# Down-projection weight sums moved from VectorE to copies and accumulating DMAs inside DRAM

## The chip, the core and the metric

The kernel runs on one core of a Trainium2 chip. The metric is the device time of one execution in microseconds. Of the kernel before, three runs gave a median of 1559.25 us (1559.11 to 1559.95). One more execution was profiled, and all views quoted here are of that one.

## The reference

Two layers over 512 tokens and 1024 channels, all in float32. The down-projection at the end of each layer is what the change touches.

```
for l in range(DEPTH):                       # DEPTH = 2
    h = _rmsnorm(x, g_mix[l])
    proj = h @ w_in[l]                       # 1024 -> 6656: gates and the inputs of four branches
    y_a, y_b, y_c, y_d = conv, neighbourhood, dilated and window attention branches (256 wide each)
    branch = jnp.einsum('bsnc,ncd->bsnd', ys, w_branch[l])
    mixed = jnp.sum(gates * branch, axis=2)
    x = x + mixed @ w_out[l]
    # ConvFFN: norm, up-projection to 2 x 2816, conv of width 3, SwiGLU, down-projection
    x = x + _conv_ffn(_rmsnorm(x, g_ffn[l]), w_up[l], ffn_conv_w[l], ffn_conv_b[l], w_down[l])
return x
```

## The kernel before, in words

Every product is made from two parts of each operand (a rounded "hi" and the remainder "lo") in three matmuls per tile. Weights come from one packed DRAM tensor `W`. `weights` loads a unit of 128x1024 into `w_raw` from SP's queue; ScalarE (ACT) makes `w_hi` from it and VectorE (DVE) makes `w_lo`. Two or three units are in hand at a time, so the matrix engine (PE) lives from what ACT and DVE have just converted.

A layer has these stages: a mixing stage (token-major projections for the three attentions, the conformer's GLU, the gates and branches, with attention and convolution steps run beside them by `tick`), the output projection, and the feed-forward stage (`ffn`, then `down`). The norm's reciprocal root `rstd` is needed in two layouts. `finish_norm` turns it: `row<-rstd` writes it to DRAM (L358), `raw<-row` reads it back broadcast to all partitions (L362), and ACT copies it to `RB` (L366). Both DMAs are issued from GpSimd's (POOL's) queue. The other early work of POOL is the rotary embedding of the dilated attention's queries and keys (`qk_stats`, L510 to L513), which DVE then scales (L519).

`down` is a fast matrix product of Winograd's kind: of the 22 tiles of `w_down` it takes pairs, 11 of them (NP2), each pair with four 512-wide blocks b11, b12, b21, b22, and needs four sums of these blocks beside the blocks themselves. `load_quad` (L971) loads a pair's 1 MB with two DMAs from POOL into `quad`; `weight_sums` (L975 to L984) makes four subtractions on DVE in the feed-forward stage and stores the four results `sums` to DRAM, 256 KB each, again from POOL. `last_units` lists what `down` loads as weights: `quad(j, q)` from `W` and `sums(j, a, b)` from that scratch.

The program's order on each engine is set by a scheduler ahead of time; on the chip an engine runs its own list in order. `issue_after(last_mm)`, which `tick` uses around side work, ties only the instructions that run on the engine of `last_mm`, which is PE.

Of the kernel before, what the change touches and what calls it, by code (L numbers as in the profile page):

```python
# [14 lines left out]
F32 = mybir.dt.float32  # L15
# [3 lines left out]
ALU = mybir.AluOpType  # L19
# [3 lines left out]
P = 128  # L23
L = 2
D = 1024
S = 512
# [3 lines left out]
NF = DFF // P  # L30

NP2 = NF // 2

EARLY = (3, 6, 10, 13, 17, 20)
EPS = 1e-6
# [153 lines left out]
class Trunk:  # L189
# [482 lines left out]
        return wait()  # L672


    def attention(self, kind, V, yi):


        nc = self.nc
        v = nc.vector
# [103 lines left out]
        es, n = {}, len(items)  # L783
# [106 lines left out]
    def ffn(self, l, last):  # L890
        nc = self.nc
        v = nc.vector
        U = []
        for i in range(4):
            u = self.conv_tile(f"U{i}")
            nc.gpsimd.memset(u[:, 0:1], 0.0)
            nc.gpsimd.memset(u[:, 513:514], 0.0)
            U.append(u)
        F, self.got = [], {}
        self.load_quad(l, 0)  # L900
        for i in range(NF):
            ys, pss = [], []
            for s in range(2):
                pss.append(self.mm())
                self.block(pss[s])
                self.tick()
            if i % 2 == 0:

                with self.tc.issue_after(self.last_mm.ins):
                    self.weight_sums(l, i // 2)  # L910
            for s in range(2):
                c = i + s * NF
                ps = pss[s]
                u = U[(2 * i + s) % 4]
                v.tensor_tensor(u[:, 1:513], ps, self.RB, ALU.mult)  # L915
                y = self.fp.tile([P, S], F32, name=f"cy{s}", tag=f"cy{s}", bufs=2)
                w = lambda t: self.par('ffn_conv_w', c * 3 + t)
                nc.scalar.activation(y, u[:, 1:513], AF.Identity, scale=w(1), bias=self.par('ffn_conv_b', c))  # L918
                v.scalar_tensor_tensor(y, u[:, 0:512], w(0), y, ALU.mult, ALU.add)  # L919
                v.scalar_tensor_tensor(y, u[:, 2:514], w(2), y, ALU.mult, ALU.add)  # L920
                ys.append(y)
                if s == 0:
                    si = self.fp.tile([P, S], F32, name="fth", tag="fth", bufs=2)
                    nc.scalar.activation(si, y, AF.Silu)  # L924
                    ys[0] = si
            f = ys[1]
            if last and i % 2 == 1 and i // 2 < KT:
                self.turn_res(i // 2)

            fl = self.fp.tile([P, S], F32, name=f"fl{i}", tag=f"fl{i}", bufs=1)  # L930
            v.tensor_tensor(fl, f, ys[0], ALU.mult)
            F.append(fl)
            if i in EARLY:
                self.split_pair(F, EARLY.index(i), self.got)
        return F
# [19 lines left out]
    def last_units(self, l):  # L955

        quad = lambda j, q: self.quads[l][j][:, q * S:(q + 1) * S]
        sums = lambda j, a, b: self.sums[l][j][:, a * S:b * S]
        units = []
        for j in range(NP2):  # L960
            units.append(lambda j=j: [quad(j, 0), sums(j, 0, 1)])
            units.append(lambda j=j: [sums(j, 1, 3)])
        for f in (lambda j: quad(j, 2), lambda j: sums(j, 3, 4), lambda j: quad(j, 3)):
            units.extend(lambda f=f, js=js: [f(j) for j in js] for js in PHASES)
        self.w_list.extend((0, u) for u in units)

    def load_quad(self, l, j):

        self.quad = [self.fp.tile([P, 1024], F32, name="quad", tag="w_more", bufs=2) for _ in range(2)]
        for q in range(2):  # L970
            self.nc.gpsimd.dma_start(self.quad[q], self.quads[l][j][:, q * 1024:(q + 1) * 1024])  # L971

    def weight_sums(self, l, j):

        v = self.nc.vector  # L975
        (b11, b12), (b21, b22) = ((t[:, :S], t[:, S:]) for t in self.quad)
        t3, t2 = (self.fp.tile([P, S], F32, name=n, tag=n, bufs=1) for n in ("t3", "t2"))
        self.after_mm(v.tensor_tensor(t3, b22, b12, ALU.subtract))  # L978
        v.tensor_tensor(b12, b12, b11, ALU.subtract)
        v.tensor_tensor(t2, b22, b12, ALU.subtract)  # L980
        v.tensor_tensor(b21, b21, t2, ALU.subtract)
        self.sums[l][j] = self.dram.tile([P, 4 * S], F32, name=f"sums{j}", tag=f"sums{j}", bufs=1)
        for n, t in enumerate((t2, b12, t3, b21)):
            self.nc.gpsimd.dma_start(self.sums[l][j][:, n * S:(n + 1) * S], t)  # L984
        if j + 1 < NP2:
            self.load_quad(l, j + 1)

    def pair_tags(self, j):

# [15 lines left out]
    def split_pair(self, F, j, got):  # L1005

        nc = self.nc
        v = nc.vector
        fi, fk = F[2 * j:2 * j + 2]

        def tile(t):
            pool = self.xpool if t[:2] in ("xh", "xl") else self.fp
            return pool.tile([P, S], F32R, name=f"p{t}", tag=t, bufs=2 if t in ("lo", "xr", "xn", "cy0", "cy1") else 1)

        tags = self.pair_tags(j)
        ih, kh, il, kl, ah, al = (tile(t) for t in tags[:6])
        if j % 2 == 0:
            got['b'] = [tile(t) for t in tags[6:]]
        lo, hi = slice(0, 256), slice(256, 512)
        bh, bl = (t[:, (lo, hi)[j % 2]] for t in got['b'])  # L1020
        a = self.fp.tile([P, S], F32, name="sum", tag="xr" if j < len(EARLY) else "fth", bufs=2)

        def split(h, l, x):
            nc.scalar.activation(h, x, AF.Copy)
            v.tensor_tensor(l, x, h.bitcast(F32), ALU.subtract)

        v.tensor_tensor(a[:, lo], fi[:, hi], fk[:, hi], ALU.add)
        v.tensor_tensor(fi[:, hi], fi[:, lo], fi[:, hi], ALU.subtract)
        v.tensor_tensor(a[:, hi], a[:, lo], fi[:, lo], ALU.subtract)
        split(ih, il, fi)  # L1030
        split(ah, al, a)
        split(kh, kl, fk)
        v.tensor_tensor(fk[:, lo], fk[:, lo], a[:, hi], ALU.subtract)
        split(bh, bl, fk[:, lo])
        cut = lambda h, l, c: [(h[:, c + b * P:c + (b + 1) * P], l[:, c + b * P:c + (b + 1) * P]) for b in range(2)]
        got[j] = {'a11': cut(ih, il, 0), 's3': cut(ih, il, 256), 'a12': cut(kh, kl, 0), 'a22': cut(kh, kl, 256),
                  's1': cut(ah, al, 0), 's2': cut(ah, al, 256), 's4': cut(bh, bl, 0)}

    def down(self, F, last):
        nc = self.nc  # L1040
        v = nc.vector
# [20 lines left out]
        tags = [f"U{i}" for i in range(4)] + ["cy0", "cy1"] * 2  # L1062
        xt = {(b, h): self.conv_tile(tags[4 * h + b])[:, :S] for h in range(2) for b in range(NB)}
        if last:
            for b, h in ((2, 1), (3, 1), (0, 1), (1, 1), (2, 0), (3, 0), (0, 0), (1, 0)):
                nc.sync.dma_start(xt[b, h], self.resT[b * P:(b + 1) * P, h * S:(h + 1) * S])
            u = [self.fp.tile([P, S], F32, name="xn", tag="xn", bufs=2) for _ in range(2)]
        else:
            u = [xt[0, 1], xt[1, 1]]

            xr = [self.load_res(d, self.fp, f"e{d}" if d < 6 else "xr") for d in range(KT)]

        def add(t, x):
            v.tensor_tensor(t, t, x, ALU.add)
# [2 lines left out]
            nc.scalar.activation(u[b], A[b], AF.Copy)  # L1077
        for b in range(2):
            add(u[b], B[b])
        for b in range(2):  # L1080
            if last:
                add(xt[2 + b, 1], C[b])
            else:
                v.tensor_tensor(xt[2 + b, 1], u[b], C[b], ALU.add)
            add(xt[2 + b, 1], E[b])
        if last:
            for b in range(2):
                for t in (xt[2 + b, 1], xt[2 + b, 0], xt[b, 1]):
                    add(t, u[b])
                self.store(xt, 2 + b, 1)  # L1090
        for banks, x, n, h in ((A, 'a12', 0, 0), (E, 'a22', 2, 0), (C, 's4', 0, 1)):

            whole = len(PHASES) - 2 * (banks is C)
            for js in PHASES[:whole]:
# [8 lines left out]
            for b in range(2):  # L1103
# [4 lines left out]
                if last or banks is C:  # L1108
                    with self.first():
                        add(t, banks[b])  # L1110
                elif banks is E:
                    v.tensor_tensor(t, u[b], banks[b], ALU.add)
                else:
                    nc.scalar.activation(t, banks[b], AF.Copy)
                if last:
# [23 lines left out]
    def run(self):  # L1139
        nc, tc = self.nc, self.tc  # L1140
        with ExitStack() as st:
# [5 lines left out]
            self.psum = pool("psum", space=PSUM)  # L1147
            self.dram = pool("dram", space=bass.MemoryType.DRAM)
            self.w_list = []
            self.quads, self.sums = [], []  # L1150
            for l in range(L):
                off, quads = 0, []
                for kind, _, n in UNITS:
# [4 lines left out]
                    else:  # L1158
                        self.w_list.append((n, lambda src=src: [src]))
                self.quads.append(quads)  # L1160
                self.sums.append([None] * NP2)
                self.last_units(l)
            self.w_emitted = self.w_used = 0
            self.first_hi = None
# [45 lines left out]
    def layer(self, l):  # L1210
# [3 lines left out]
        with tc.tile_pool(name="gate", bufs=1, reuse_waits="tile") as self.gp:  # L1214
            with tc.tile_pool(name="attn", bufs=1, reuse_waits="tile") as self.ap:
# [5 lines left out]
                with self.first():  # L1221
                    for _ in self.qk_stats(Q, 4, 4, None):
# [3 lines left out]
                self.tabs = [None] * 4  # L1226
                self.queue(chain(self.na_biases(l, 3 if l else 5), self.qk_norm(Q, 4, 4, 0),
                                 self.attention('na', V, 1)))
                Vd = self.new_V()
                self.project_v(V, Vd)  # L1230
                Q = self.project_qk()
# [96 lines left out]
```

## Time and profile before

| what | value |
|---|---|
| median of three runs | 1559.25 us |
| profiled execution, first to last instruction (its span, the only time it has) | 1556.7 us |
| PE busy | 1550.7 us |
| DVE busy | 1235.9 us |
| ACT busy | 834.7 us |
| POOL busy | 174.8 us |
| PE's granted clock, mean | 0.999 |
| bytes moved by DMA | 244.86 MB, 46.67 MB of it from POOL's queue |

The median is 2.55 us above the span, which is taken as what lies around the instructions. A busy time is the sum of an engine's instruction times; PE's matmuls overlap each other, so its busy share says that it always had work, not that it ran at its peak.

### The profile page before, as it was taken

What the parts mean: (1) busy time and instruction counts of PE and PEld (TensorE: products, weight loads), DVE (VectorE), ACT (ScalarE), POOL (GpSimd) and SP (SyncE); (2) the same over time, 40 slices, a digit from 0 to 9 for tenths busy, and PEclk for the clock granted to TensorE, in tenths of its full rate; (3) what the DMA queues carried; (4) which work ended last, traced back from release to release, by engine and by line L of the source; (5) the groups of instructions that cost most, each with busy time, mean ns of one, the idle gap of its engine ahead of it and who ended that gap; (6) DMA issues with size and microseconds to landing.
All of it is one profiled execution on the core that took longest, in us unless ns stands there. A gap on an engine that the chain in (4) does not pass through costs nothing.

```text
span 1556.7 us, 20353 instructions
## 1 busy us (share of the span) xinstructions
PE 1550.7 (100%) x7122; PEld 1287.2 (83%) x7122; DVE 1235.9 (79%) x2102; ACT 834.7 (54%) x1420; POOL 174.8 (11%) x304
## 2 busy tenths in 40 slices
PE   9999999999999999999999999999999999999999
PEld 8888888888888888888888888888888888888887
DVE  6689988765689997796676899887656899977964
ACT  6778767333445443364457787672434444443643
POOL 0102002122001111100001020022120111111000
PEclk9999999999999999999999999999999999999999
DMA  7632222222645555576555422223226667655674
GB/s 236 192 93 87 83 81 82 95 98 93 215 162 203 192 187 187 202 238 211 188 181 184 117 72 87 74 76 108 95 95 211 194 221 238 202 203 191 219 231 165
DMA packets 103382, 244.86 MB, mean 157 GB/s; under 512 B 27504, under 2 KB 29424, under 8 KB 103280
## 3 DMA queue, kind: packets, MB, share of 16 engines
q1 hardware_dynamic: 89392, 196.37, 39.6%
q0 software_dynamic: 13600, 46.67, 8.5%
q8 instruction: 56, 0.92, 0.2%
q10 hardware_dynamic: 288, 0.52, 0.1%
q14 instruction: 46, 0.38, 0.1%
HBM read 202.63 MB, written 35.66 MB: 153 GB/s over the span
## 4 chain that ended last, share of the span: by engine, by line
PE 94%; DVE 3%; ACT 3%; issue 0%; ACTq 0%; DVEq 0%
PE mm L243 22%; PE mm L244 22%; PE mm L245 22%; PE aux L1048 3%; PE aux L1047 3%; PE aux L1046 3%; PE mm L467 2%; PE mm L469 2%; PE mm L468 2%; PE mm L1047 2%; PE mm L1048 2%; PE mm L1046 2%; PE aux L760 2%; PE aux L737 2%; PE aux L467 1%; PE aux L469 1%
## 5 line engine op out<-in xcount | busy, mean ns | idle before, releaser
L222 ACT ACTIVATE w_hi<-w_raw 128x1024 fp32r<-128x1024 f32 (+1 forms) x305 | 318.6, 1045 | 382.6 <-PE mm L244 218.9
L243 PE MATMUL mm<-xh,w_hi 128*128 128x512 f32 x1280 | 499.5, 390 | 0.0
L244 PE MATMUL mm<-xl,w_hi 128*128 128x512 f32 x1280 | 498.6, 390 | 0.0
L245 PE MATMUL mm<-xh,w_lo 128*128 128x512 f32 x1280 | 498.6, 390 | 0.0
L224 DVE TENSOR_TENSOR w_lo<-w_raw,w_hi 128x1024 fp32r<-128x1024 f32 (+1 forms) x305 | 368.7, 1210 | 83.4 <-ACT w_hi L222 81.3
L245 PEld LDWEIGHTS mm<-xh,w_lo 128*128 128x128 f32 x1280 | 240.3, 188 | 50.7
L243 PEld LDWEIGHTS mm<-xh,w_hi 128*128 128x128 f32 x1280 | 240.3, 188 | 49.1
L244 PEld LDWEIGHTS mm<-xl,w_hi 128*128 128x128 f32 x1280 | 240.3, 188 | 48.7
L836 POOL TENSOR_TENSOR mx<-mx,t 128x512 f32<-128x512 f32 x44 | 66.9, 1530 | 428.0 <-DVE t L835 327.1
L405 DVE SCALAR_TENSOR_TENSOR cv<-cv,prm 128x512 f32<-128x512 f32 x120 | 93.8, 781 | 0.7
L915 DVE TENSOR_TENSOR U<-mm,RB 128x512 f32<-128x512 f32 x88 | 60.0, 686 | 34.9 <-PE mm L245 34.8
L918 ACT ACTIVATE cy<-U,prm 128x512 f32<-128x512 f32 x88 | 70.7, 807 | 30.1 <-DVE U L915 29.9
L806 DVE TENSOR_TENSOR t<-mm,RB 128x512 f32<-128x512 f32 x64 | 43.9, 686 | 47.0 <-PE mm L245 46.8
L467 PE MATMUL mm<-w_hi,xh 128*128 128x512 f32 x192 | 76.4, 398 | 0.4 <-DVE V L595 0.4
L468 PE MATMUL mm<-w_lo,xh 128*128 128x512 f32 x192 | 75.0, 390 | 0.0
L469 PE MATMUL mm<-w_hi,xl 128*128 128x512 f32 x192 | 74.8, 390 | 0.0
L724 ACT ACTIVATE e<-e,rl 128x256 f32<-128x256 f32 (+2 forms) x96 | 57.3, 597 | 21.8 <-DVE rl L723 21.5
L920 DVE SCALAR_TENSOR_TENSOR cy<-U,prm,cy 128x512 f32<-128x512 f32 x88 | 65.5, 746 | 1.3
L919 DVE SCALAR_TENSOR_TENSOR cy<-U,prm,cy 128x512 f32<-128x512 f32 x88 | 65.3, 744 | 0.6 <-ACT cy L918 0.6
L924 ACT ACTIVATE fth<-cy 128x512 f32<-128x512 f32 x44 | 27.8, 632 | 64.1 <-DVE cy L920 64.0
L984 POOL DMA_DIRECT2D sums<-t x44 | 23.9, 544 | 339.4 <-DVE t L978 311.3
L717 ACT ACTIVATE e<-e,nm 128x256 f32<-128x256 f32 (+2 forms) x96 | 57.6, 600 | 2.7
(300 smaller groups left out, 2605.2 us busy)
## 6 DMA issues: line engine op xcount, KB each, us to landing
w_raw<-W SPq DMA_DIRECT2D x223, 512.0 KB, 3.5
quad<-W POOLq DMA_DIRECT2D x44, 512.0 KB, 5.3
w_raw<-W SPq DMA_DIRECT2D x66, 256.0 KB, 3.6
sums<-t POOLq DMA_DIRECT2D x44, 256.0 KB, 3.2
sums<-quad POOLq DMA_DIRECT2D x44, 256.0 KB, 3.8
w_raw<-sums SPq DMA_DIRECT2D x44, 256.0 KB, 3.8
w_raw<-sums SPq DMA_DIRECT2D x22, 512.0 KB, 4.4
res<-xn SPq DMA_DIRECT2D x24, 256.0 KB, 2.0
```

The source lines that it names most:

```text
L222: w = nc.scalar.activation(hi[:, s], raw[:, s], AF.Copy)
L224: nc.vector.tensor_tensor(lo[:, s], raw[:, s], hi[:, s].bitcast(F32), ALU.subtract)
L243: mm(ps, lhsT=wh, rhs=xh, start=start, stop=False)
L244: mm(ps, lhsT=wh, rhs=xl, start=False, stop=False)
L245: self.last_mm = mm(ps, lhsT=wl, rhs=xh, start=False, stop=stop)
L405: self.after_mm(v.scalar_tensor_tensor(acc, u[:, t:t + S], w(t), acc, ALU.mult, ALU.add))
L467: mm(pss[b], lhsT=self.Xh[k][:, t], rhs=hi[:, s], start=k == 0, stop=False)
L468: mm(pss[b], lhsT=self.Xh[k][:, t], rhs=lo[:, s], start=False, stop=False)
L469: self.last_mm = mm(pss[b], lhsT=self.Xl[k][:, t], rhs=hi[:, s], start=False, stop=k == KT - 1)
L1046: mm(ps, lhsT=x[0], rhs=w[0][:, cols], start=start, stop=False, skip_group_check=again)
L1047: mm(ps, lhsT=x[0], rhs=w[1][:, cols], start=False, stop=False, skip_group_check=again)
L1048: self.last_mm = mm(ps, lhsT=x[1], rhs=w[0][:, cols], start=False, stop=stop, skip_group_check=again)
```

## The change

The loads into `quad`, the four subtractions on DVE and the stores of `sums` are removed from the feed-forward stage. In their place, `weight_sums` becomes a generator of 24 DMAs in each layer, all issued from POOL, DRAM to DRAM. The 11 pairs are cut in three chunks of 4, 4 and 3 (CHUNK), so that a DMA moves 512 or 384 rows of 2 KB, 1.05 or 0.79 MB. Column by column, for each chunk: s3 = b12 and s1 = b11 are copied, b11 is accumulated onto s3 and b21 onto s1, then s3 is copied to s2 and b21 accumulated onto it, and s2 is copied to s4 and b22 accumulated onto it. That is 12 copies and 12 accumulating DMAs a layer. The generator is put on the list of side work in the mixing stage through `slowly`, which yields 12 times before it and twice after each DMA. The scratch `sums` has two buffers, so that the two layers do not share one. Since only additions are made, the signs in `split_pair` and `down` change and some blocks change places; the number of matmuls stays as it was.

```diff
+CHUNK = 4
+SLOW = 2
...
+    def slowly(self, g):
+        for _ in range(12):
+            yield
+        for _ in g:
+            for _ in range(SLOW):
+                yield
...
-        self.load_quad(l, 0)
...
-            if i % 2 == 0:
-                with self.tc.issue_after(self.last_mm.ins):
-                    self.weight_sums(l, i // 2)
...
-            units.append(lambda j=j: [quad(j, 0), sums(j, 0, 1)])
+            units.append(lambda j=j: [quad(j, 1), sums(j, 0, 1)])
             units.append(lambda j=j: [sums(j, 1, 3)])
...
+    def weight_sums(self, l):
+        add = self.nc.gpsimd.dma_start
+        items = []
+        for c in range(0, NP2, CHUNK):
+            n = min(CHUNK, NP2 - c)
+            t = self.dram.tile([n * P, 4 * S], F32, name=f"sums{c}", tag=f"sums{c}", bufs=2)
+            self.sums[l].append(t)
+            src = self.all_quads[l][c * P:(c + n) * P]
+            part = lambda x, i: x[:, i * S:(i + 1) * S]
+            items.append((part, t, src))
+        s2, s1, s3, s4 = range(4)
+        b11, b12, b21, b22 = range(4)
+        for d, s in ((s3, b12), (s1, b11)):
+            for part, t, src in items:
+                add(part(t, d), part(src, s))
+                yield
+        for d, s in ((s3, b11), (s1, b21)):
+            for part, t, src in items:
+                add(part(t, d), part(src, s), accum_op=ALU.add)
+                yield
+        for d, b, s in ((s2, s3, b21), (s4, s2, b22)):
+            for part, t, src in items:
+                add(part(t, d), part(t, b))
+                yield
+            for part, t, src in items:
+                add(part(t, d), part(src, s), accum_op=ALU.add)
+                yield
...
-        v.tensor_tensor(fk[:, lo], fk[:, lo], a[:, hi], ALU.subtract)
+        v.tensor_tensor(fk[:, lo], fk[:, lo], a[:, hi], ALU.add)
...
+                self.side.append(self.slowly(self.weight_sums(l)))
```

What this makes of the engines' lists is seen at three places. The first is the head of POOL's list, around layer 0's turn of `rstd`. Before, it reads:

```order
L378 MEMSET cv 128x15
L358 DMA row<-rstd 128x4 [waits DVE_49]
L362 DMA raw<-row 128x512 [waits DMAHW1_49,DMASW0_49,DMAHW2_49,PE_49,Activation_49]
L510 ISA
L510 TENSOR_TENSOR rA<-Q,rc_389 128x64 [waits Activation_49]
```

Only four memsets stand ahead of these rows. Now the same two DMAs read as follows (a DMASW wait is a wait for an earlier DMA of POOL's queue to land; sums_773 to sums_775 are layer 0's three chunks, sums_7948 to sums_7950 layer 1's; L993 are first copies, L997 first accumulations, L1001 later copies, L1004 later accumulations):

```order
L997 DMA sums_7948<-W 512x512
L997 DMA sums_7949<-W 512x512 [waits DMASW7_49]
L997 DMA sums_7950<-W 384x512 [waits DMASW0_49]
L997 DMA sums_7948<-W 512x512 [waits DMASW3_49,DMASW1_49]
L997 DMA sums_7949<-W 512x512 [waits DMASW4_49,DMASW2_49]
L997 DMA sums_7950<-W 384x512 [waits DMASW5_49]
L1001 DMA sums_7948<-sums_7948 512x512 [waits DMASW6_49]
L362 DMA row<-rstd 128x4 [waits DVE_49]
L1001 DMA sums_7949<-sums_7949 512x512 [waits DMASW7_49]
L1001 DMA sums_7950<-sums_7950 384x512 [waits DMASW0_49]
L1004 DMA sums_7948<-W 512x512 [waits DMASW4_49]
L366 DMA raw<-row 128x512 [waits DMASW5_49,DMAHW1_49,DMASW1_49,DMAHW2_49,PE_49,Activation_49]
```

Forty of the 48 DMAs of the sums, all 24 of layer 0 and 16 of layer 1, have moved ahead of `raw<-row` (now L366), 37 of them ahead of `row<-rstd` (now L362). None of the first six, nor any later one, waits for PE.

The second place is where POOL goes over to the rotary embedding (now L514); the last DMAs of layer 1's sums stand just ahead of it:

```order
L1001 DMA sums_7949<-sums_7949 512x512 [waits DMASW2_49]
L1001 DMA sums_7950<-sums_7950 384x512 [waits DMASW3_49]
L1004 DMA sums_7948<-W 512x512 [waits DMASW4_49]
L1004 DMA sums_7949<-W 512x512 [waits DMASW5_49]
L1004 DMA sums_7950<-W 384x512 [waits DMASW6_49,DMASW1_49]
L514 ISA
L514 TENSOR_TENSOR rA<-Q,rc_389 128x64 [waits Activation_49]
```

So all 48 have moved ahead of the first rotary step of layer 0.

The third place is ACT's list around `RB` (now L370):

```order
L604 ACTIVATE Q<-aux,rstd 128x512
L505 ACTIVATE sqq<-Q 128x512
L370 ACTIVATE RB<-raw 128x512
L226 ACTIVATE w_hi<-w_raw 128x1024 x2
L547 ACTIVATE KH<-aux,qg 64x512 x2
L598 ACTIVATE pt<-mm,rstd 128x4x64
```

Nothing moved there: apart from line numbers it is the order of before, as are PE's, DVE's and SP's in the mixing stage of layer 0, and the conversions of weights stand behind `RB`.

More of the change, by code (lines that the diff above doesn't have):

```diff
@@ L957, in last_units, with sums @@
         quad = lambda j, q: self.quads[l][j][:, q * S:(q + 1) * S]
-        sums = lambda j, a, b: self.sums[l][j][:, a * S:b * S]
+        def sums(j, a, b):
+            c = j // CHUNK
+            return self.sums[l][c][(j - c * CHUNK) * P:(j - c * CHUNK + 1) * P, a * S:b * S]
         units = []
         for j in range(NP2):
-            units.append(lambda j=j: [quad(j, 0), sums(j, 0, 1)])
+            units.append(lambda j=j: [quad(j, 1), sums(j, 0, 1)])
             units.append(lambda j=j: [sums(j, 1, 3)])
-        for f in (lambda j: quad(j, 2), lambda j: sums(j, 3, 4), lambda j: quad(j, 3)):
+        for f in (lambda j: quad(j, 3), lambda j: quad(j, 2), lambda j: sums(j, 3, 4)):
@@ L964, in last_units @@
             units.extend(lambda f=f, js=js: [f(j) for j in js] for js in PHASES)
         self.w_list.extend((0, u) for u in units)
[L967 to L986, printed above, removed]
+    def weight_sums(self, l):
[25 more added lines that the diff above has]
+                yield
@@ L1025, in split @@
             v.tensor_tensor(l, x, h.bitcast(F32), ALU.subtract)
-        v.tensor_tensor(a[:, lo], fi[:, hi], fk[:, hi], ALU.add)
+        v.tensor_tensor(a[:, lo], fi[:, hi], fk[:, hi], ALU.subtract)
         v.tensor_tensor(fi[:, hi], fi[:, lo], fi[:, hi], ALU.subtract)
@@ L1032, in split_pair @@
         split(kh, kl, fk)
-        v.tensor_tensor(fk[:, lo], fk[:, lo], a[:, hi], ALU.subtract)
+        v.tensor_tensor(fk[:, lo], fk[:, lo], a[:, hi], ALU.add)
         split(bh, bl, fk[:, lo])
         cut = lambda h, l, c: [(h[:, c + b * P:c + (b + 1) * P], l[:, c + b * P:c + (b + 1) * P]) for b in range(2)]
-        got[j] = {'a11': cut(ih, il, 0), 's3': cut(ih, il, 256), 'a12': cut(kh, kl, 0), 'a22': cut(kh, kl, 256),
-                  's1': cut(ah, al, 0), 's2': cut(ah, al, 256), 's4': cut(bh, bl, 0)}
+        got[j] = {'a11': cut(ih, il, 0), 's1': cut(ih, il, 256), 'a12': cut(kh, kl, 0), 's4': cut(kh, kl, 256),
+                  's3': cut(ah, al, 0), 's2': cut(ah, al, 256), 'a22': cut(bh, bl, 0)}
     def down(self, F, last):
@@ L1064, in down @@
         if last:
-            for b, h in ((2, 1), (3, 1), (0, 1), (1, 1), (2, 0), (3, 0), (0, 0), (1, 0)):
+            for b, h in ((2, 0), (3, 0), (0, 0), (1, 0), (2, 1), (3, 1), (0, 1), (1, 1)):
                 nc.sync.dma_start(xt[b, h], self.resT[b * P:(b + 1) * P, h * S:(h + 1) * S])
@@ L1068, in down @@
         else:
-            u = [xt[0, 1], xt[1, 1]]
+            u = [xt[2, 1], xt[3, 1]]
             xr = [self.load_res(d, self.fp, f"e{d}" if d < 6 else "xr") for d in range(KT)]
@@ L1079, in down, with less @@
             add(u[b], B[b])
+        def less(t, x):
+            v.tensor_tensor(t, t, x, ALU.subtract)
         for b in range(2):
+            t = xt[2 + b, 0]
             if last:
-                add(xt[2 + b, 1], C[b])
-            else:
-                v.tensor_tensor(xt[2 + b, 1], u[b], C[b], ALU.add)
-            add(xt[2 + b, 1], E[b])
+                less(t, C[b])
+                add(t, E[b])
+            else:
+                v.tensor_tensor(t, u[b], C[b], ALU.add)
+                v.tensor_tensor(t, E[b], t, ALU.subtract)
         if last:
             for b in range(2):
[L1088 to L1091, printed above, removed]
+                less(xt[2 + b, 0], u[b])
+                less(xt[b, 0], u[b])
+                add(xt[2 + b, 1], u[b])
+                self.store(xt, 2 + b, 0)
+        for banks, x, n, h in ((A, 'a12', 0, 1), (E, 'a22', 0, 0), (C, 's4', 2, 1)):
             whole = len(PHASES) - 2 * (banks is C)
@@ L1111, in down @@
                 elif banks is E:
-                    v.tensor_tensor(t, u[b], banks[b], ALU.add)
+                    v.tensor_tensor(t, banks[b], u[b], ALU.subtract)
                 else:
@@ L1149, in run @@
             self.w_list = []
-            self.quads, self.sums = [], []
+            self.quads, self.sums, self.all_quads = [], [], []
             for l in range(L):
@@ L1160, in run @@
                 self.quads.append(quads)
-                self.sums.append([None] * NP2)
+                self.sums.append([])
+                self.all_quads.append(self.W[l, off - NP2 * 2048 * P:off].rearrange("(p c) -> p c", c=2048))
                 self.last_units(l)
```

## The prediction

> **What bounds the kernel now.** I read the page's first and fourth parts, then PE's waits, then windows by stage.
>
> ```profile
> span 1556.7 us, 20353 instructions
> PE 1550.7 (100%) x7122; PEld 1287.2 (83%) x7122; DVE 1235.9 (79%) x2102; ACT 834.7 (54%) x1420; POOL 174.8 (11%) x304
> ...
> PE 94%; DVE 3%; ACT 3%; issue 0%; ACTq 0%; DVEq 0%
> ...
> PE aux L1179 <- DVE warm L1176: 1.2, 1, 1.2
> PE mm L467 <- DVE V L595: 0.4, 1, 0.4
> PE aux L537 <- DVE KL L544: 0.3, 1, 0.3
> PE aux L699 <- DVE pt L745: 0.3, 1, 0.3
> ...
> 0.00:38.90 38.90, 37.72 (x169) 31.70 (x170) 26.33 (x61) 23.65 (x35) 1.66 (x10) 1.00 0.73 236
> 38.90:73.20 34.30, 33.91 (x164) 27.85 (x163) 24.07 (x53) 22.69 (x46) 0.00 (x0) 1.00 0.69 203
> 395.00:790.00 395.00, 395.00 (x1760) 327.32 (x1759) 318.78 (x460) 184.67 (x237) 35.92 (x70) 1.00 0.60 199
> ```
>
> The chain that ended last is 94% PE, and in 1556.7 us PE waits for four things, 2.2 us together. A windows row gives the stretch, the busy time of PE, PEld, DVE, ACT and POOL, the granted clock, the DMA engines' share and GB/s. In the feed-forward stage of layer 0 (395 to 790 us), where the old sums are made, PE is busy 395.00 of 395 us. Nothing that leaves DVE there can shorten it by more than those waits, of which none lies there. So the time is PE's work plus whatever new waits the change gives PE, and these must be looked for where the DMAs were put.
>
> **What is removed.** Per layer 11 groups of four subtractions on DVE, and over both layers 44 DMAs that load `quad` and 88 that store `sums`.
>
> ```profile
> L978 DVE TENSOR_TENSOR t<-quad 128x512 f32<-128x512 f32 x22 | 15.0, 683 | 0.0
> L979 DVE TENSOR_TENSOR quad<-quad 128x512 f32<-128x512 f32 x22 | 15.0, 683 | 0.0
> L980 DVE TENSOR_TENSOR t<-quad 128x512 f32<-128x512 f32 x22 | 15.0, 682 | 0.0
> L981 DVE TENSOR_TENSOR quad<-quad,t 128x512 f32<-128x512 f32 x22 | 15.0, 682 | 0.0
> ```
>
> That is 60.0 us of DVE over both layers, all beside a PE that is never idle: gain on the path 0. The other edits of `split_pair`, `down` and `last_units` swap signs and blocks with as many matmuls, tensor operations and bytes loaded: 0, within a microsecond at the tail.
>
> **What the moved DMAs do to POOL's queue.** Without a tie to PE the 24 DMAs of each layer are held only by each other. All of layer 0's and 16 of layer 1's stand ahead of `raw<-row`. The scheduler put them there by its own clock; on the chip POOL runs its list in order and waits where it must, as this row shows (POOL sat idle until an earlier DMA of `sums` had landed), and with it everything behind.
>
> ```profile
> 452.41 0.54 POOL L971 DMA_DIRECT2D quad<-W  x1 [0.81 <-DMA sums<-quad]
> ...
> 32.27 0.68 POOL L358 DMA_DIRECT2D row<-rstd  x1 [31.30 <-DVE rstd L277]
> 35.48 0.55 POOL L362 DMA_DIRECT2D raw<-row  x1 [2.54 <-ACT Q L600]
> 73.20 0.32 POOL L510 TENSOR_TENSOR rA<-Q,rc 128x64 f32<-128x64 f32 x1 [37.17 <-ACT Q L600]
> ...
> 38.91 1.13 ACT L366 ACTIVATE RB<-raw 128x512 f32<-128x512 f32 x1 [1.33 <-DMA raw<-row]
> 39.93 1.05 ACT L222 ACTIVATE w_hi<-w_raw 128x1024 fp32r<-128x1024 f32 x1
> 44.87 1.06 ACT L222 ACTIVATE w_hi<-w_raw 128x1024 fp32r<-128x1024 f32 x1 [3.88 <-PE mm L469]
> 45.84 0.67 ACT L543 ACTIVATE KH<-aux,qg 64x512 fp32r<-64x512 f32 x1
> ...
> 54.49 0.47 PE L467 MATMUL mm<-w_hi,xh 128*128 128x512 f32 x1 [0.39 <-DVE V L595]
> ```
>
> Timeline rows give start and duration in us and, in brackets, the idle time ahead and its releaser. ACT waits at L366 for `raw` already before (1.33 us), and stands there with all that follows: the next `w_hi` and the evacuations. PE has weights for the projection it is in, and stops at the row of 54.49, which needs ACT. So PE will stand until `raw` lands.
>
> **When `raw` lands.** Its descriptors go through POOL's DMA queue behind 40 DMAs. One column of a layer is 11 x 128 x 512 x 4 bytes = 2.884 MB. Ahead of `raw` are seven columns of copies, 20.19 MB, and six columns and one chunk (1.05 MB) of accumulations, 18.35 MB.
>
> ```profile
> q1 hardware_dynamic: 89392, 196.37, 39.6%
> q0 software_dynamic: 13600, 46.67, 8.5%
> ...
> raw<-row POOLq DMA_DIRECT2D x2, 256.0 KB, 3.4
> sums<-t POOLq DMA_DIRECT2D x44, 256.0 KB, 3.2
> ```
>
> q0 is POOL's queue: 8.5% of 1556.7 us on all 16 engines for 46.67 MB is 2.83 us per MB, between DRAM and SBUF. No DMA of the trace goes from DRAM to DRAM, and none accumulates. Bounds: a copy costs one such pass if reading and writing overlap fully, two if they don't. An accumulation, which reads two streams and writes one, costs one to four. Nothing in the trace lies nearer to one end, so I take the middles, 1.5 and 2.5. Below one I exclude both, since each byte of a copy is moved at least once.
>
> - copies: 20.19 x 2.83 x 1.5 = 85.7 us (57.1 to 114.3)
> - accumulations: 18.35 x 2.83 x 2.5 = 129.8 us (51.9 to 207.7)
> - SP's own loads up to the hold: 0.73 x 38.9 = 28.4 us of the same engines
> - `raw` to landing: 3.4 us
>
> The Trainium skill (DMA: Bandwidth & Descriptors, section Latency and other measured facts) gives 214 GB/s as the full rate of copies between HBM tensors. By it the copies would take 94 us instead, and the sum below 9 us more; no run here shows it yet.
>
> Waits of a microsecond or three between dependent DMAs are covered, since two other chunks are under way. SP's loads are slowed meanwhile, as both queues want the engines; PE reaches the hold later, but the hold outlasts that. `RB` can start at 85.7 + 129.8 + 28.4 + 3.4 = 247.3 us instead of 38.9: 208.4 late. While ACT catches up, PE gets back what it ran ahead: ACT has this much work from `RB` to PE's stop,
>
> ```profile
> 38.90:54.50 15.60, 15.21 (x77) 12.46 (x75) 13.37 (x29) 11.16 (x18) 0.00 (x0) 1.00 0.49 152
> ...
> 82.76 0.32 POOL L513 TENSOR_TENSOR Q<-rA,rB 128x64 f32<-128x64 f32 x1
> 89.06 0.68 DVE L519 TENSOR_TENSOR Q<-Q,r_y 128x512 f32<-128x512 f32 x1
> ```
>
> 11.2 of 15.6 us, so the loss is 208.4 - 4.4 = 204.0 us.
>
> **A second hold.** The eight last DMAs stand ahead of the rotary step, which before begins 34.3 us after `RB`. POOL is through once 1.84 MB of accumulations (13.0 us) and 2.88 MB of copies (12.2) are done, beside SP's loads of that window (0.69 x 34.3 = 23.7) and one landing (3.2): 52.1 us. Cover: 34.3 - 4.4, plus the 6.0 us by which the rotary step ends before DVE needs it (83.1 to 89.06): 35.9. So DVE, and with it `w_lo` and PE, stands about 16.2 us more (4.4 at the lower bounds, 28 at the upper). After that the three last accumulations are beside work that needs the DMA engines to a third, and layer 1, whose sums are then done, finds an empty POOL queue: 0.
>
> **Sum.** 1556.7 + 204.0 + 16.2 = 1776.9 us of span, and the median was 2.55 above the span: 1779. At the lower bounds 140.8 - 38.9 - 4.4 + 4.4 = 101.9, so 1661, and 1657 without a second hold. At the upper ones 353.8 - 43.3 + 28 = 338.5, so 1898.
>
> **The rivals.**
> 1. *Accumulations are as cheap as loads.* If the DMA engines read two streams and write one at the rate of a load, and copies too, PE is held 100 us at `RB`: 1655 to 1700. For it: the rate of q0 above is with landings of only 256 and 512 KB. Against: three accesses for one.
> 2. *Accumulations are far dearer* (four passes and more): 1850 to 1900, and beyond 1900 past 4.1 passes or so. It is the open side, since nothing here measures them.
> 3. *The sums are out of the way in time, so it is not slower.* All that is ahead of `raw` would have to be through the queue by 35.48 us, 38.5 MB beside SP's loads. That decides at 1080 GB/s. The first 38.9 us, in 40 slices, moved
>
> ```profile
> GB/s 0 24 196 345 396 282 388 356 397 407 331 299 194 276 314 190 335 264 332 131 135 375 166 17 181 175 232 320 315 328 379 282 135 251 246 0 0 42 177 211
> ```
>
> at most 407 GB/s. In that case the time is 1559, with the 60 us of DVE work gone where nobody waits for DVE. It also covers the change not doing what it says: a POOL that doesn't stand at its waits.
> 4. *Hidden in part*: queue order lets `raw` overtake what is queued in other rings, and only the waits in POOL's own list count, up to the copy two rows ahead of `raw`. The three DMAs after it (about 1 MB accumulated, 1.8 MB copied) then don't count: 15 us less. It lies within the main range.
>
> **How the numbers follow.** The hold at `RB` with middling prices (1700 to 1850): 0.60. Rival 1: 0.16. Rival 2 up to 1900: 0.09, above: 0.08. Something between 1563 and 1655: 0.04. Rival 3: 0.03, two thirds of it within 0.2% and the rest faster. 0.2% (3 us) is about what a measurement of this kernel can tell from no change. The range from 1655 to 1900 takes in both bounds and holds 0.85. Slower has 0.97, same 0.02, faster 0.01.
>
> **What would show it.** In the profile after, `raw<-row` should be issued near 240 us instead of 35.48, ACT should have one idle stretch of some 200 us ahead of `RB`, ended by that DMA, and PE one that begins near 54 us or, with slower loads at the start, a little later. The DMA engines should be 90% busy or more in it, with q0 as the main queue. A second, short wait of DVE should stand at L519's successor. In the feed-forward windows PE should stay at 100%, with DVE some 30 us less busy in each layer. The second layer should take as long as before. I am wrong if ACT's wait for `raw` is short or PE goes on through it, if the time from the first DMA of the sums to `raw` is not DMA work but waiting between DMAs, or if PE also waits in a later stage.

## The result, and the profile after

The changed kernel takes 1717.62 us (median of four runs, 1716.43 to 1718.36), against 1559.32 us for the kernel before on the same chip. The ratio is 1.1015, with a 95% interval of 1.0999 to 1.1031. The profiled span went from 1556.7 to 1715.7 us, 159.0 us more.

The page's first and fourth parts, after:

```profile
span 1715.7 us, 19999 instructions
PE 1568.9 (91%) x7122; PEld 1297.0 (76%) x7122; DVE 1193.8 (70%) x2014; ACT 833.0 (49%) x1420; POOL 142.8 (8%) x220
...
PE 82%; DMA 7%; issue 6%; DVE 3%; ACT 2%; POOL 1%; SPq 0%; POOLq 0%; DVEq 0%; ACTq 0%
```

PE was idle for 6 us of its span before and is now idle for 147 us of a longer one. The chain that ended last, which had no DMA among its shares, now has 7% of it, and another 6% in which the profile shows no releaser. PE's waits (total, times, longest):

```profile
PE mm L471 <- DVE V L599: 119.7, 2, 119.0
PE aux L541 <- DVE Q L523: 4.7, 4, 4.2
PE aux L712 <- DMA KL<-KL: 4.5, 1, 4.5
```

One wait of 119.0 us makes three quarters of the loss. The timeline says where it comes from; its rows are POOL's, ACT's and PE's, in that order:

```profile
158.81 0.66 POOL L1001 DMA_DIRECT2D sums<-sums  x1 [4.07 <-issue]
159.45 0.60 POOL L362 DMA_DIRECT2D row<-rstd  x1
...
179.15 1.06 POOL L1004 DMA_DIRECT2D sums<-W  x1 [14.72 <-DMA row<-rstd]
179.84 0.97 POOL L366 DMA_DIRECT2D raw<-row  x1
...
214.54 0.94 POOL L1004 DMA_DIRECT2D sums<-W  x1 [2.33 <-DMA sums<-sums]
...
230.83 0.32 POOL L514 TENSOR_TENSOR rA<-Q,rc 128x64 f32<-128x64 f32 x1 [15.35 <-ACT Q L604]
...
192.28 1.11 ACT L370 ACTIVATE RB<-raw 128x512 f32<-128x512 f32 x1 [127.28 <-DMA raw<-row]
...
199.26 0.77 PE L471 MATMUL mm<-w_hi,xh 128*128 128x512 f32 x1 [118.98 <-DVE V L599]
```

`raw<-row` is issued at 179.84 us instead of 35.48. ACT stands 127 us ahead of `RB`, which begins at 192.28 instead of 38.91, 153.4 us late. PE goes on to 80.3 us with the weights it has and then stands until ACT and DVE have evacuated its banks. By the rotary step the delay is 157.6 us (230.83 against 73.20), and from the GLU on it stays at 159. The last row of POOL's sums is through at 215.5 us, and POOL then waits 15.35 us for `Q`: there was no second hold. Windows (columns as before):

```profile
100.00:190.00 90.00, 0.00 (x0) 0.00 (x0) 0.00 (x0) 0.00 (x0) 18.52 (x26) 0.50 1.02 223
199.30:205.00 5.70, 4.95 (x11) 3.44 (x12) 4.96 (x9) 4.33 (x9) 0.59 (x1) 0.50 1.03 368
220.00:230.00 10.00, 10.00 (x51) 8.30 (x50) 4.06 (x12) 6.81 (x18) 0.00 (x0) 1.00 1.10 268
555.00:950.00 395.00, 395.00 (x1760) 327.45 (x1759) 297.60 (x416) 184.52 (x239) 0.24 (x4) 1.00 0.44 141
```

From 100 to 190 us nothing computes and the DMA engines are full. The last row is the feed-forward stage of layer 0, shifted by about 160 us: 395.00 of 395 us for PE and 1760 matmuls on record, exactly as before, with DVE 21 us less busy. The work that was taken off DVE bought nothing. Over the whole span DVE's busy time fell by 42.1 us, not by the 60.0 that the removed instructions' durations add up to. Most of the gap is a matter of counting: the durations of all DVE instructions add up to 1345.2 us before and 1288.4 after, 56.8 less, but a busy time counts only once the stretch in which one instruction overlaps the next (the L978 row of 444.73 us lasts 0.68, and the next one starts at 445.33). So the busy times here are somewhat less than the plain sum of the instruction times.

The two new kinds of DMA can be priced in stretches where only one of them is under way and SP's queue stands. The first pair of rows is 104 to 109 us (copies), the second 140 to 150 us (accumulations):

```profile
DMA packets 469, 1.80 MB, mean 360 GB/s; under 512 B 30, under 2 KB 30, under 8 KB 469
q0 software_dynamic: 469, 1.80, 102.2%
...
DMA packets 962, 2.01 MB, mean 201 GB/s; under 512 B 29, under 2 KB 29, under 8 KB 962
q0 software_dynamic: 962, 2.01, 109.4%
```

That is 2.78 us per MB copied and 4.97 us per MB accumulated, or 0.98 and 1.76 of the 2.83 us that POOL's loads and stores between DRAM and SBUF cost before. The first two are elapsed time, while 2.83 is time on the 16 engines; with the shares of 102.2% and 109.4% the time on the engines is 2.84 and 5.44 us per MB, 1.00 and 1.92 of such a pass.

### The profile page after: what moved, and what is told of

It is laid out like the page before. It is cut to its first block, busy times and chain, and to the rows that moved or that the text cites. A ratio compares the mean times of both kernels' runs of the same rounds, so it can differ in the third digit from the quotient of the medians.

```text
span 1715.7 us, 19999 instructions
## 1 busy us (share of the span) xinstructions
PE 1568.9 (91%) x7122; PEld 1297.0 (76%) x7122; DVE 1193.8 (70%) x2014; ACT 833.0 (49%) x1420; POOL 142.8 (8%) x220
## 4 chain that ended last, share of the span: by engine, by line
PE 82%; DMA 7%; issue 6%; DVE 3%; ACT 2%; POOL 1%; SPq 0%; POOLq 0%; DVEq 0%; ACTq 0%
PE mm L247 20%; PE mm L249 20%; PE mm L248 20%; PE aux L1066 2%; PE aux L1067 2%; PE aux L1065 2%; DMA sums<-sums 2%; DMA sums<-W 2%; PE mm L1066 2%; PE mm L1067 2%; PE mm L1065 2%; PE mm L471 2%; PE mm L473 2%; PE mm L472 2%; PE aux L772 1%
## 5 line engine op out<-in xcount | busy, mean ns | idle before, releaser
L471 PE MATMUL mm<-w_hi,xh 128*128 128x512 f32 x192 | 80.5, 419 | 122.9 <-DVE V L599 119.7
L471 PEld LDWEIGHTS mm<-w_hi,xh 128*128 128x128 f32 x192 | 38.2, 199 | 132.0 <-issue 121.6
L472 PE MATMUL mm<-w_lo,xh 128*128 128x512 f32 x192 | 78.8, 410 | 0.5 <-DVE w_lo L228 0.5
L473 PE MATMUL mm<-w_hi,xl 128*128 128x512 f32 x192 | 77.9, 407 | 0.0
L370 ACT ACTIVATE RB<-raw 128x512 f32<-128x512 f32 x2 | 2.2, 1112 | 128.6 <-DMA raw<-row 128.6
```

What stands on the lines that cost most here:

```text
L471: mm(pss[b], lhsT=self.Xh[k][:, t], rhs=hi[:, s], start=k == 0, stop=False)
L472: mm(pss[b], lhsT=self.Xh[k][:, t], rhs=lo[:, s], start=False, stop=False)
L473: self.last_mm = mm(pss[b], lhsT=self.Xl[k][:, t], rhs=hi[:, s], start=False, stop=k == KT - 1)
```

## The experiments

**All copies.** The same DMAs in the same order with the same waits, but none accumulates, so that no sum is formed.

```diff
-                add(part(t, d), part(src, s), accum_op=ALU.add)
+                add(part(t, d), part(src, s))
```

> The changed kernel with every accumulating DMA of the sums replaced by a plain copy of the same bytes, so that no sum is formed; order and waits stay. Theory (the hold at RB is the DMA work queued ahead of raw, at the prices that the trace of the changed kernel shows: 2.78 us per MB copied, 4.97 us per MB accumulated): 18.35 MB x 2.19 us = 40 us come out, about 1677 us. By the prediction's middles (1.5 and 2.5 load passes) 52 us, 1666. Rival (the time is waits between dependent DMAs, which remain): 1700 to 1718.

Measured: 1672.31 us, 45.3 us less than the change. ACT's row at `RB`:

```profile
146.69 1.11 ACT L370 ACTIVATE RB<-raw 128x512 f32<-128x512 f32 x1 [79.23 <-DMA raw<-row]
```

`RB` comes 45.6 us earlier than in the changed kernel, and the whole time follows it. Most of that is the difference in price; some 5 us are that `raw` itself lands sooner, 7.6 us after its issue (139.11 us) instead of 12.4. The rival, that the time was waits between dependent DMAs, is out. The measured time lies between the two sums (1677 and 1666) and doesn't decide between them by itself; the windows above do.

**The sums behind `raw`.** Each DMA of the sums is queued behind the layer's `raw<-row` in POOL's list, which `issue_after` does when it is given an instruction of POOL.

```diff
-            nc.gpsimd.dma_start(raw, row.unsqueeze(0).broadcast_to([P, S]))
+            self.last_pool = nc.gpsimd.dma_start(raw, row.unsqueeze(0).broadcast_to([P, S])).ins
...
-        add = self.nc.gpsimd.dma_start
+        def add(*a, **k):
+            with self.tc.issue_after(self.last_pool):
+                self.nc.gpsimd.dma_start(*a, **k)
```

> The sums' DMAs of each layer are tied behind raw<-row of that layer in POOL's list, so that RB is not held, but they still stand ahead of the rotary step. Theory (whatever POOL does next is held until all but the last of its queued DMAs have landed): in each layer the rotary step starts near 36 + 80 + 28 us after the layer's start instead of 73, PE stands some 60 to 70 us in both layers, 1670 to 1715 us in all, about as slow as the change. Rival (only RB's wait matters, the rotary step has slack): under 1575.

Measured: 1676.94 us. `RB` begins at 40.7 us (38.91 before), and the hold is at the next thing that POOL has to do. POOL's and DVE's rows, and PE's longest wait:

```profile
141.46 0.95 POOL L982 DMA_DIRECT2D sums<-W  x1 [0.83 <-DMA sums<-sums]
142.16 0.69 POOL L514 TENSOR_TENSOR rA<-Q,rc 128x64 f32<-128x64 f32 x1
...
144.35 0.69 DVE L523 TENSOR_TENSOR Q<-Q,r_y 128x512 f32<-128x512 f32 x1 [37.76 <-POOL Q L517]
```

```profile
PE aux L711 <- DVE pt L757: 75.3, 4, 40.6
```

The rotary step starts at 142.16 us, the moment POOL has issued its last accumulation, instead of 73.20. It happens in both layers: the second `RB` is 61.3 us late (869.9 against 808.6), which is layer 0's loss, and layer 1 adds 56.0 to make 117.3 us of span. So the wait at `RB` isn't special. Whatever stands behind the DMAs in POOL's list waits for them.

**Layer 1's sums later.** Layer 0 as in the change; layer 1's DMAs are tied to the last POOL instruction written before each of them (its `raw`, a rotary step, or a sum of the branches). The lines that note this instruction in `last_pool` are those shown with the run above and the one below.

```diff
...
+            if l:
+                with self.tc.issue_after(self.last_pool):
+                    self.nc.gpsimd.dma_start(*a, **k)
+            else:
+                self.nc.gpsimd.dma_start(*a, **k)
```

> Layer 0's 24 DMAs stand ahead of raw as in the change; layer 1's 24 are tied to POOL's own work in the mixing stage of layer 1. Theory: raw is ready after 11.5 MB of copies (32 us), 11.5 MB of accumulations (57 us), SP's loads (28) and its landing (12), 129 us, so RB is some 91 us late instead of 153 and the whole about 1656 us. Rival (layer 1's DMAs among them cost nothing because they fill gaps): 1700 to 1718.

Measured: 1645.94 us, 10 us under the 1656 expected.

```profile
127.26 1.11 ACT L370 ACTIVATE RB<-raw 128x512 f32<-128x512 f32 x1 [63.38 <-DMA raw<-row]
```

With 24 instead of 40 DMAs ahead of it, `RB` begins at 127.26 us; the sum at the measured prices gave 129. That it comes so close is in part luck: the sum put 12 us for the landing of `raw`, which took 3.5, and `raw` was issued 7 us later (123.78) than the other terms say. The lateness, 88.4 us, is the whole loss (87.3 us of span), where the expectation had some 6 us more behind `RB`. The 16 DMAs of layer 1 that the scheduler had put among layer 0's first work cost the other 72 us, 65 of them ahead of `RB`.

**Paced.** Both layers tied as layer 1 was in the run above, so that a DMA can't run ahead of the POOL work written before it.

```diff
...
+                self.last_pool = g.tensor_tensor(Qv[b][:, :, 8:16], A[:, :H, 8:16], B[:, :H, 0:8], ALU.add).ins
...
+        r = (v if n == ORDER[3] and d >= 6 else nc.gpsimd).tensor_tensor(m, m, t, ALU.add)
+        if not (n == ORDER[3] and d >= 6):
+            self.last_pool = r.ins
...
+            with self.tc.issue_after(self.last_pool):
+                self.nc.gpsimd.dma_start(*a, **k)
```

> Every DMA of the sums is tied behind the last POOL instruction written before it (raw, a rotary step or a sum of the branches), so that the generator's pace holds on POOL's list. Theory (the loss is the place in POOL's list, and nothing waits for the DVE work that was taken away): the same as before within 4 us, 1557 to 1563. Rival (DMAs inside DRAM crowd out the weight loads wherever they stand): 1580 or more. Rival (the DVE work taken out of the feed-forward stage pays once the hold is gone): 1550 or less.

Measured: 1562.42 us, 1.0020 of before (1.0011 to 1.0029). The hold is gone with the same 48 DMAs. What is left is 3.4 us of median and 4.2 of span. Most of it is lost by the first rotary step of each layer, which comes at 75.02 and 853.72 us, against 73.20 and 849.85 before. PE's part of it shows in two windows:

```profile
39.00:60.00 21.00, 19.26 (x92) 15.31 (x91) 16.91 (x32) 12.31 (x20) 0.00 (x0) 1.00 0.87 273
790.00:850.00 60.00, 58.61 (x277) 48.19 (x276) 38.84 (x87) 35.53 (x67) 3.06 (x5) 1.00 0.79 246
```

PE is busy 1.35 us less in the first and 1.4 less in the second than in the run below, with the DMA engines at 0.87 and 0.79.

**Paced, and later.** As the last, but the generator is put on the list only after the rotary step of the window attention.

```diff
-                self.side.append(self.slowly(self.weight_sums(l)))
...
                 ready = self.beside(self.qk_stats(Q, 4, 2, 2))
+                self.side.append(self.slowly(self.weight_sums(l)))
```

> As the paced version, but the sums begin only behind the rotary step of the window attention, so that no DMA of theirs runs beside the turn of the values through DRAM (39 to 60 us of a layer). Theory (the 3 to 4 us that the paced version lost come from its first copies beside those short transfers): 1558 to 1560. Rival (they come from the DMAs' load on the weight stream in general): 1562 or more; the sums then run beside the gates and POOL's adds wait for them.

Measured: 1558.90 us, 1.0001 of before (0.9993 to 1.0010).

```profile
39.00:60.00 21.00, 20.61 (x99) 16.76 (x98) 17.74 (x33) 13.74 (x24) 0.00 (x0) 1.00 0.57 163
790.00:850.00 60.00, 60.00 (x289) 49.87 (x289) 39.54 (x90) 38.85 (x74) 1.51 (x3) 1.00 0.63 192
```

The two windows are as in the kernel before. In the first one the paced version had only its first three copies under way (issued from 35.84 us on, the next DMA of the sums at 78.73), and here none is. So its loss came from the first copies beside the transfers of that stretch, and not from the sums' load in general, which is here too, only later. Which of the transfers was late stays open.

**No sums at all.** The kernel before without its sums: `down` loads blocks where it would load sums.

```diff
-        self.load_quad(l, 0)
...
-                    self.weight_sums(l, i // 2)
...
-        sums = lambda j, a, b: self.sums[l][j][:, a * S:b * S]
+        sums = lambda j, a, b: self.quads[l][j][:, a * S:b * S]
```

> The kernel before without load_quad and weight_sums: down loads blocks of the weights where it would load their sums, so the sums aren't made at all, neither on DVE nor by DMA. It bounds what any other place for them can gain. Theory (PE never waits for that work): within 2 us of before, 1557 to 1561. Rival (the 60 us of DVE work or the DMA traffic hold PE in a way that its waits don't show): 1550 or less.

Measured: 1558.60 us, 1.0000 of before (0.9991 to 1.0010).

```profile
395.00:790.00 395.00, 395.00 (x1760) 327.47 (x1759) 297.42 (x416) 183.75 (x238) 0.44 (x8) 1.00 0.43 141
```

PE does in the feed-forward stage what it did with the sums beside it. Without the sums the kernel isn't faster, so no other place for them can win more than the noise. The later paced version is as fast as the kernel before and as a kernel without sums; no version tried is faster than these by more than the noise.

## Why the prediction was right, and where its sizes were off

The mechanism came out as forecast. The DMAs weren't held to PE's pace, POOL's list held `raw<-row`, ACT stood at `RB`, PE ran out of evacuated banks (from 80.3 us on, 26 us later than the 54 that was named), and the feed-forward stage gave nothing back. The time, 1717.6 us, lies within the range and within the likeliest case's 1700 to 1850, but 61 us below the 1779 that was named. By the prediction's steps:

- *Copies, 85.7 us:* mis-sized. At 2.78 us per MB they took 56.1. The price is the lower bound, one load pass, not the middle. The Trainium skill's 214 GB/s for copies between HBM tensors (DMA: Bandwidth & Descriptors, section Latency and other measured facts), given there for 16 KiB rows from the sync and scalar queues, doesn't hold for these copies from POOL; the trace has 360 GB/s, and the measurement decides.
- *Accumulations, 129.8 us:* mis-sized. At 4.97 us per MB they took 91.2, at 1.76 load passes instead of 2.5. These two terms are 68 us too high, more than the whole error. Taking the middle between far bounds was the choice that cost most. Rival 1, accumulations as cheap as loads, is refuted as well: they cost 1.8 times a copy.
- *SP's loads, 28.4 us:* right in size. In the first 100 us its queue took 25.0% of the engines:

```profile
q1 hardware_dynamic: 4032, 8.72, 25.0%
```

- *`raw` to landing, 3.4 us:* 12.4, since it queues behind an accumulation just issued (at 179.15 us). That one landed at 191.65 and `raw` at 192.24, so `raw` overtook nothing, and rival 4 is out.
- *Waits between dependent DMAs, "covered":* not all of them. POOL stood 14.72 us ahead of the accumulation of 179.15 and issued nothing. The row names `row<-rstd`, which landed last (178.85 us), but by POOL's list this accumulation waits for DMASW4 and only `raw<-row` behind it for DMASW5. What the accumulation needs by the program is the copy of 158.81 us into the same column, which landed at 178.71. The same step of layer 0 waited as long for its copy, with no `row<-rstd` near it:

```profile
79.18 1.04 POOL L1004 DMA_DIRECT2D sums<-W  x1 [13.94 <-DMA sums<-sums]
```

  So it was a wait between dependent DMAs; `raw<-row` would have had to wait for `row<-rstd` as long in any case. In layer 0 the DMA engines moved at least 238 GB/s meanwhile (65 to 80 us). Here, in 40 slices of 2.25 us from 100 us on, the DMA engines moved

```profile
GB/s 259 280 375 344 259 218 224 167 162 205 208 208 224 279 266 328 296 198 207 198 196 207 205 206 196 197 194 205 205 216 275 267 292 323 148 57 97 154 188 201
```

  and fell to 57 GB/s in the slice from 178.75 to 181.0 us, in which the wait ended: the queue had run nearly dry. The terms as measured are 56.1 + 91.2 + 25.0 + 12.4 us. The last accumulation ahead of `raw`, 5.2 us at its price, is in two of them, so they make 179.5 us, against 192.28 for `RB`. Of the other 12.8 us this gap is 3 to 5 and the start of the first DMA 1.25; the rest stays open.
- *PE runs ahead, 4.4 us back:* about right, but lost again. PE stopped a little ahead of the row of 54.49: 32 groups of three matmuls into `mm` (L471 to L473) stand ahead of its restart at 199.26, and 35 (L467 to L469) ahead of 54.49. The counterpart of that row is

```profile
204.32 0.63 PE L471 MATMUL mm<-w_hi,xh 128*128 128x512 f32 x1
```

  12.0 us after `RB` began where it was 15.6 before, so 3.5 us came back. But from there to the rotary step 26.5 us passed instead of 18.7. In that stretch PE's granted clock fell again (0.71 from 210 to 215 us, 0.61 from 215 to 220), and transfers took longer beside the sums still running: `KL<-KL` landed in 11.4 us (median of the first 260 us) instead of 3.9, and PE waited 4.5 us for one. Together that is a loss of 4.3 us, not a gain.
- *The second hold, 16.2 us:* didn't happen. POOL was through 23.2 us after `RB` began and not 52.1. Two of the eight DMAs counted there were issued before `RB` began (181.94 and 183.73 us), all were cheaper, and SP's queue took 28.4% of the 23.2 us, 6.6 us where 23.7 were counted. The run with the sums behind `raw` shows that the place can hold, when more stands ahead of it.
- *Layer 1 costs nothing, the edits of `down` cost nothing:* right. The delay is 159 us at layer 0's GLU and at the end.

## What to carry to other kernels

Transfers without a tie to the engine whose pace they should follow went to the front of their queue in this kernel's schedule, and POOL, which runs its list in order and waited for them, held everything else on it. Before such work is moved, look for the first small thing behind it that another engine needs. Moving work off an engine for which nobody waits was worth nothing, and a run with that work left out tells so at once. Where two new kinds of transfer carry the sum, the middle of wide bounds is a guess; its error was more than the whole error here.

## What was not expected of the hardware

A copy inside DRAM in rows of 2 KB ran at 360 GB/s, as fast as POOL's loads and stores of SBUF in the trace before (2.83 us per MB, 353 GB/s), and the accumulating DMA at 201 GB/s of result. Issuing a DMA of that size from POOL took 0.62 to 0.64 us for a copy and 1.02 to 1.04 us for an accumulation (medians of the four source lines). After its stand PE began at a granted clock of 0.50 and kept it for 5.7 us, with 0.63 us a matmul, where 0.39 is usual at full clock. The Trainium skill (TensorE: Matmul & The Clock Gate, section Part 1: The HAM clock gate) describes such a half-rate start after idleness, of about 3.4 us of sustained work; in this trace it lasted longer, with short waits of PE in it. After PE's wait of 4.25 us that ended at 69.27 us the matmuls ran at half rate for 5.9 us too, with no wait above 0.16 us in between.
